# A third pair of k-tiles by seven products in ten of the eleven FFN blocks of a hybrid decoder kernel

## The chip, the cores and the metric

One core of one Trainium2 chip. The metric is device microseconds of one execution. The kernel before takes 1394.79 us, the median of three runs (1393.06 to 1396.41).

## What is computed

One layer: a pre-norm, a combined input projection, differential attention beside a state-space branch, a gated merge, an output projection, and then the feed-forward part (FFN) that the change touches. All is float32; x is 256 tokens by 2048, the FFN is 5632 wide.

```
z = _rms_norm(h, norm_ffn_pre[l])
f = (jax.nn.silu(z @ w_ffn_gate[l]) * (z @ w_ffn_up[l])) @ w_ffn_down[l]
h = h + _rms_norm(f, norm_ffn_post[l])
```

## The kernel before

**Split matmuls.** TensorE works on float32r. Each operand is held as a high part and a low part, and each product is three matmuls of 128x128 by 512 columns: high by high, high by low, low by high. The split of a weight tile is a CAST on ScalarE (`hi`) and a subtraction on VectorE (`lo`).

**FFN blocks.** The 5632 columns are eleven blocks of 512, `ffn0` to `ffn10`. A block multiplies z (two token tiles, 16 k-tiles of 128) by a 128x1024 weight tile per k-tile: 512 columns of gate, 512 of up. A plain k-tile (kind `D`) takes four products, 12 matmuls.

**Pairs by seven products.** In `ffn1` to `ffn10` two neighbouring k-tiles, with the two token tiles and the two column halves, can be seen as a 2x2 by 2x2 block product, and that can be done with seven products in place of eight (21 matmuls in place of 24), if sums of the blocks are made first. The sums of z are made once, by `combos`, near the end of `ffn0`. The sums of the weights are made in each block by `do_sums` on VectorE: one subtraction of 1024 columns (t1 and t3), then t2 and t4 of 512. A pair is four entries of the list `SETS`: `R2` (second tile), `B1` (first half of the first tile), `T13` and `T24` (the sums), in this order. P1 to P7 are the products' accumulators. Since plain k-tiles feed the same accumulators, a plain tile is a product each into P4, P5, P2 and P3, with the difference of the two token tiles of z (`hold["cd"]`) for P3.

**Buffers.** A pair's two weight tiles land in `ga[:, 1]`, and there is one such buffer; the sums go to `ga[:, 0]`, also one. A new pair isn't loaded before the last pair's `B1` has been split (`state["pair"]`), and what of the buffer is free is loaded at once, so the first quarter goes behind the first sum and the last behind `B1` or t4. Plain tiles land in four `raw` buffers. There are five pairs of `hi` and `lo` buffers, and the splits run up to four entries ahead of the products (`ensure`). All these copies are issued by SyncE (SP).

**Order.** The code is written in one order, but in the FFN blocks (`unpin`) a scheduler orders each engine's instructions at build time; each engine then runs its own list in order. Accumulators of odd and of even blocks lie in different PSUM banks (`s_alloc`), so the order differs between the two and repeats every two blocks. At a block's end `s_evac` adds the accumulators up on VectorE (seven adds of 512 columns) with two gate products behind a SiLU on ScalarE; `hid_t` transposes the result on TensorE.

Of the kernel before, what the change touches and what calls it, by code (L numbers as in the profile page):

```python
# [89 lines left out]
def hybrid_block_kernel(  # L90
# [52 lines left out]
    def big8(dtype=F32, shape=(P, 2048)):  # L143
        return b8.tile(list(shape), dtype, tag="b8", name=nm("b8"))
# [297 lines left out]
    hold = {}  # L442
# [540 lines left out]
    def add(*a, **kw):  # L983
        b = Block(*a, **kw)
        if b.order is None:
            b.order = bank_order(b.nk)
        blocks.append(b)
        return b
# [246 lines left out]
    def zf(t):  # L1235
        return ga[:, t].rearrange("p a (k n) -> p (a k) n", n=P)

    def combos(cb):

        if cb == 0:  # L1240
            cs = big8(F32R, (P, 2, 4, 2, P))
            hold["cs"], hold["cd"] = (cs[:, 0], cs[:, 1]), [big8(F32R, (P, 16, P)) for _ in range(2)]
        z0, z1 = zf(0), zf(1)
        n = 2 if cb % 2 else 4
        k0, k1, k2 = 4 * cb, 4 * cb + 2, 4 * cb + 3
        tt = V.tensor_tensor
        (ch, cl), (dh, dl) = hold["cs"], hold["cd"]
        tt(z1[:, k0:k0 + n], z0[:, k0:k0 + n], z1[:, k0:k0 + n], op=ALU.subtract)
        parts = [(z1[:, k0:k0 + n], dh[:, k0:k0 + n], dl[:, k0:k0 + n])]
        if n == 2:  # L1250
            tt(z1[:, k2], z1[:, k1], z1[:, k2], op=ALU.add)
            tt(z1[:, k1], z0[:, k1], z1[:, k1], op=ALU.subtract)
            tt(z0[:, k1], z1[:, k2], z0[:, k1], op=ALU.subtract)
            tt(z0[:, k2], z0[:, k2], z0[:, k1], op=ALU.subtract)
            parts += [(z1[:, k1:k1 + 2], ch[:, 0:2, cb // 2], cl[:, 0:2, cb // 2]),
                      (z0[:, k1:k1 + 2], ch[:, 2:4, cb // 2], cl[:, 2:4, cb // 2])]
        for src, h, l in parts:
            A.copy(h, src)
            tt(l, src, h.bitcast(F32), op=ALU.subtract)
# [53 lines left out]
    def load_ffn(b):  # L1313
        def f(k, r):
            for w, c0 in ((w_g, 0), (w_u, 512)):
                nc.sync.dma_start(r[:, :, c0:c0 + 512],
                                  w[k * P:(k + r.shape[1]) * P, b * 512:(b + 1) * 512].rearrange("(a p) c -> p a c", p=P))
        return f
# [33 lines left out]

    quad = lambda k: [(kind, k) for kind in ("R2", "B1", "T13", "T24")]
    plain = lambda *ks: [("D", k) for k in ks]
    SETS = plain(0, 1, 2, 3, 4) + quad(6) + plain(5, 8, 9, 10) + quad(14) + plain(11, 12, 13)
    USES = dict(D=(("P4", 0), ("P5", 1), ("P2", 0), ("P3", 1)), R2=(("P2", 0), ("P3", 1)), B1=(("P1", 0),),
                T13=(("P7", 1), ("P5", 0)), T24=(("P6", 0), ("P4", 1)))

    def s_mm(m, accs, h, l, first, last):
        n, key, c = m  # L1360
        kind, k = SETS[n]
        (ch, cl), (dh, dl) = hold["cs"], hold["cd"]
        z = lambda k_, t: tuple(zT[i][:, k_, t * P:(t + 1) * P] for i in "hl")
        q = k // 8
        if kind == "D":
            xh, xl = dict(P4=z(k, 1), P5=z(k, 1), P2=z(k, 0), P3=(dh[:, k], dl[:, k]))[key]
        elif key in ("P1", "P2", "P4"):
            xh, xl = dict(P1=z(k, 0), P2=z(k + 1, 0), P4=z(k + 1, 1))[key]
        else:
            i = dict(P7=0, P5=1, P6=2, P3=3)[key]  # L1370
            xh, xl = ch[:, i, q], cl[:, i, q]
        ps, sl = accs[key], slice(c * 512, c * 512 + 512)
        T.matmul(ps, xh, h[:, sl], start=first, stop=False)
        T.matmul(ps, xh, l[:, sl], start=False, stop=False)
        T.matmul(ps, xl, h[:, sl], start=False, stop=last)

    def s_alloc(b):
        def f():
            wide = side2()
            acc = lambda: acc_pool.tile([P, 512], F32, tag="acc", name=nm("acc"))  # L1380
            d = {}
            if b % 2:
                for key in ("P4", "P5", "P2", "P3"):
                    d[key] = acc()
                d["P1"], d["P6"], d["P7"] = side(), wide[:, 0, :], wide[:, 1, :]
            else:
                d["P4"], d["P5"], d["P2"] = wide[:, 0, :], wide[:, 1, :], side()
                for key in ("P1", "P6", "P7", "P3"):
                    d[key] = acc()
            return d  # L1390
        return f

    def s_evac(b):
        def f(key, accs):
            s0, s1, X, Y = (hold["sc"][:, 512 * n:512 * n + 512] for n in range(4))
            plus = lambda o, a, k_: V.tensor_tensor(o, a, accs[k_], op=ALU.add)

            def gated(t, g, u):
                A.activation(g, g, AF.Silu, scale=hold["rstd2"][:, t:t + 1])
                V.scalar_tensor_tensor(g, u, hold["rstd2"][:, t:t + 1], g, op0=ALU.mult, op1=ALU.mult)  # L1400
                hid[(b, t)] = g
            if key == "P1":
                A.copy(s0, accs["P1"])
            elif key == "P6":
                plus(X, s0, "P6")
                plus(Y, X, "P7")
            elif key == "P4":
                plus(s1, Y, "P4")
            elif key == "P5":
                plus(X, X, "P5")  # L1410
                plus(Y, Y, "P5")
                gated(1, s1, Y)
            elif key == "P2":
                plus(s0, s0, "P2")
            elif key == "P3":
                plus(X, X, "P3")
                gated(0, s0, X)
                tasks.append((f"hid{b}", hid_t(b)))
        return f

    every = [[(n, key, c) for key, c in USES[kind]] for n, (kind, _) in enumerate(SETS)]
    s_order = [st[:3] for st in every[:3]] + [[st[3] for st in every[:3]]] + every[3:-2]
    s_order.append([st[i] for i in range(4) for st in every[-2:]])
    for b in range(1, NB):
        add(f"ffn{b}", len(SETS), load_ffn(b), None, s_evac(b), budget=0.6, mm=s_mm, alloc=s_alloc(b), order=s_order)
        blocks[-1].sets = SETS
        blocks[-1].akey = lambda m: m[1]

    def steps(*fs):
# [13 lines left out]
        9: steps((unpin,), (h_add, 1, 3), (h_piece, 0, 2), (h_square, 0, 0)),  # L1443
        10: steps((h_piece, 1, 2), (h_square, 1, 0)),
        11: steps((h_square, 0, 1), (combos, 0)),
        12: steps((h_piece, 0, 3), (h_square, 1, 1)),
        13: steps((h_piece, 1, 3), (h_square, 0, 2), (combos, 1)),
        14: steps((h_square, 1, 2), (h_square, 0, 3), (combos, 2)),
        15: steps((h_square, 1, 3), (norm2,), (combos, 3))}

# [131 lines left out]
```

## Time and profile before

| what | value |
|---|---|
| median of three runs | 1394.79 us |
| the profiled execution, its span | 1398.8 us, 1397.0 us |
| TensorE busy | 1356.9 us, 97% |
| VectorE busy | 1009.5 us, 72% |
| ScalarE busy | 722.6 us, 52% |
| granted TensorE clock, mean | 0.983 |

The span is what the profiler sees from the first to the last instruction. Engines are PE (TensorE), PEld (its weight loads), DVE (VectorE), ACT (ScalarE), POOL and SP. In the trace all instructions of the helper `InOrder` have line 41, so they are told apart by tiles. `lo<-raw,hi` is the split of a plain tile, `lo<-ga,hi` that of a pair's entry, `ga<-ga` of 1024 columns the first sum of a pair, `ga<-ga` of 512 one of the short sums, `b<-b,acc` and `b<-b,side` the adds at a block's end. Blocks `ffn1` to `ffn10` run from about 710 to 1137 us.

### The profile page before, as it was taken

The page shows a single profiled execution, that of the slowest core. Times are in us where ns is not written, and L with a number is a line of the kernel's source. Part 1 is how long each engine was busy: PE and PEld are TensorE (multiplying, and loading weights), DVE is VectorE, ACT ScalarE, POOL GpSimd, SP SyncE. Part 2 cuts the span into 40 slices and gives each one's busy share as a digit, 9 for nine tenths or more (in the row PEclk, how much of TensorE's full clock was granted, in tenths as well). Part 3 has the DMA queues.
Part 4 walks back from the last instruction along what each step waited for, and adds up shares of the span by engine and source line. Part 5 has one row for each costly group of instructions (what it writes and reads, how often), then busy time and mean ns, then how long its engine had stood idle before and what let it go on. Part 6 is the DMA issues. An engine that isn't in the chain of part 4 may idle for free.

```text
span 1397.0 us, 17778 instructions
## 1 busy us (share of the span) xinstructions
PE 1356.9 (97%) x6307; PEld 1104.5 (79%) x6307; DVE 1009.5 (72%) x1316; ACT 722.6 (52%) x1079; POOL 168.3 (12%) x187
## 2 busy tenths in 40 slices
PE   7999999999999989999999999999999999999997
PEld 6887777777777778888788888888888878888885
DVE  4954999868999956645976777767868676555555
ACT  3646545687545454544574555545555455444443
POOL 3090344302244100000000000000000000000001
PEclk8999999999999989999999999999999999999999
DMA  8678666544566556656566656566565566555551
GB/s 244 200 225 253 212 190 186 153 136 143 176 177 187 167 175 227 223 187 197 166 193 207 211 154 229 172 200 211 175 210 189 180 248 228 189 201 180 197 181 60
DMA packets 103577, 266.72 MB, mean 191 GB/s; under 512 B 11488, under 2 KB 18480, under 8 KB 100352
## 3 DMA queue, kind: packets, MB, share of 16 engines
q1 hardware_dynamic: 102272, 260.09, 58.5%
q10 hardware_dynamic: 608, 4.20, 0.8%
q0 software_dynamic: 608, 1.30, 0.4%
q8 instruction: 49, 0.80, 0.2%
q14 instruction: 40, 0.33, 0.1%
HBM read 257.16 MB, written 8.39 MB: 190 GB/s over the span
## 4 chain that ended last, share of the span: by engine, by line
issue 53%; PE 25%; DVE 13%; POOL 3%; ACT 3%; DMA 2%; SPq 1%; POOLq 0%; DVEq 0%; ACTq 0%
PE acc L41 23%; DVE lo L41 4%; PE side L41 2%; DVE ssB L41 2%; DVE ssD L41 2%; DVE ssA L41 2%; DVE ssC L41 1%; ACT hi L41 1%; DMA b<-in_x_dram 1%; SPq L668 1%; DVE ga L41 1%; DVE sim L41 1%; DVE b L41 1%; POOL tabS L685 1%; DVE sre L41 0%
## 5 line engine op out<-in xcount | busy, mean ns | idle before, releaser
L41 DVE TENSOR_TENSOR lo<-raw,hi 128x1024 fp32r<-128x1024 f32 (+1 forms) x385 | 473.6, 1240 | 163.7 <-ACT hi L41 163.0
L41 ACT CAST hi<-raw 128x1024 fp32r<-128x1024 f32 (+1 forms) x384 | 398.0, 1050 | 318.3 <-PE acc L41 220.1
L41 PE MATMUL acc<-hi,b 128*128 128x512 f32 x596 | 209.2, 394 | 0.4 <-DVE b L41 0.3
L41 PE MATMUL acc<-lo,xT_h 128*128 128x512 f32 x512 | 205.0, 404 | 2.6 <-DVE lo L41 2.5
L41 PE MATMUL acc<-hi,xT_l 128*128 128x512 f32 x512 | 202.4, 399 | 0.0
L41 PE MATMUL acc<-hi,xT_h 128*128 128x512 f32 x512 | 164.1, 406 | 5.3 <-ACT hi L41 3.5
L41 PEld LDWEIGHTS acc<-hi,b 128*128 128x128 f32 x596 | 112.4, 189 | 24.9 <-issue 0.8
L41 PEld LDWEIGHTS acc<-lo,xT_h 128*128 128x128 f32 x512 | 98.5, 193 | 28.1 <-DVE lo L41 5.1
L41 PEld LDWEIGHTS acc<-hi,xT_h 128*128 128x128 f32 x512 | 97.2, 193 | 28.4 <-ACT hi L41 6.2
L41 PE MATMUL acc<-lo,b 128*128 128x512 f32 x298 | 117.4, 394 | 2.1 <-DVE lo L41 2.1
L41 DVE TENSOR_TENSOR lo<-ga,hi 128x1024 fp32r<-128x1024 f32 x80 | 84.6, 1087 | 47.0 <-ACT hi L41 47.0
L41 ACT CAST hi<-ga 128x1024 fp32r<-128x1024 f32 x80 | 72.7, 943 | 82.1 <-PE acc L41 71.5
L41 PEld LDWEIGHTS acc<-hi,xT_l 128*128 128x128 f32 x512 | 98.3, 192 | 19.6
L41 PE MATMUL acc<-lo,zT_h 128*128 128x512 f32 x274 | 105.8, 392 | 0.4 <-DVE lo L41 0.4
L41 PE MATMUL acc<-hi,zT_l 128*128 128x512 f32 x274 | 105.1, 390 | 0.0
L41 PE MATMUL acc<-hi,zT_h 128*128 128x512 f32 x274 | 95.4, 393 | 0.2 <-ACT zT_h L41 0.2
L41 DVE TENSOR_TENSOR ga<-ga 128x512 f32<-128x512 f32 (+4 forms) x85 | 60.5, 716 | 35.4 <-DMA ga<-in_w_ffn_gate_dram 32.2
L439 POOL TENSOR_TENSOR rstdf<-rstdfm,half 128x1 f32<-128x1 f32 x2 | 1.1, 547 | 675.3 <-DVE rstdfm L41 675.3
L41 PE MATMUL side<-lo,zT_h 128*128 128x512 f32 x210 | 82.1, 391 | 0.0
L41 PE MATMUL side<-hi,zT_l 128*128 128x512 f32 x210 | 81.8, 389 | 0.0
L41 PE MATMUL side<-hi,zT_h 128*128 128x512 f32 x210 | 77.7, 389 | 0.0
L41 DVE TENSOR_TENSOR lo<-b,hi 128x1024 fp32r<-128x1024 f32 x40 | 49.0, 1225 | 39.0 <-ACT hi L41 39.0
(230 smaller groups left out, 2326.7 us busy)
## 6 DMA issues: line engine op xcount, KB each, us to landing
raw<-in_w_in_dram SPq DMA_DIRECT2D x127, 512.0 KB, 4.2
raw<-in_w_ffn_gate_dram SPq DMA_DIRECT2D x136, 256.0 KB, 3.7
raw<-in_w_ffn_up_dram SPq DMA_DIRECT2D x136, 256.0 KB, 4.0
raw<-in_w_ffn_down_dram SPq DMA_DIRECT2D x48, 512.0 KB, 4.3
b<-in_w_ffn_down_dram SPq DMA_DIRECT2D x20, 1024.0 KB, 4.9
raw<-in_w_out_dram SPq DMA_DIRECT2D x32, 512.0 KB, 4.1
ga<-in_w_ffn_gate_dram SPq DMA_DIRECT2D x40, 256.0 KB, 3.7
ga<-in_w_ffn_up_dram SPq DMA_DIRECT2D x40, 256.0 KB, 3.0
```

The costliest lines, as they stand in the source:

```text
L41: ins = f(*a, **kw)
L439: G.tensor_tensor(r, ms, half[:, :n], op=ALU.pow)
L668: nc.sync.dma_start(stack_b[:, j // 2, n, :, j % 2].rearrange("g q o n -> q g o n"), t_[32 * j:32 * j + 32])
L685: G.tensor_tensor(up(tss), hi(sa), lo(cb), op=ALU.mult)
```

## The change

`SETS` makes k-tiles 10 and 11 a third pair in `ffn1` to `ffn10` and moves the plain tiles around the pairs. Its sums of z need a place: they go into slots 6, 7, 14 and 15 of the differences `hold["cd"]`, which no plain tile uses. `combos` makes them, and its second call of four columns of tiles becomes two differences and four sums.

```diff
+    def sums_of(k, i, n, part):
+
+        if k == 10:
+            return hold["cd"][part][:, (6, 7, 14, 15)[i]:(6, 7, 14, 15)[i] + n]
+        return hold["cs"][part][:, i:i + n, k // 8]
+
     def combos(cb):
...
-        n = 2 if cb % 2 else 4
+        n = 2 if cb else 4
...
-            parts += [(z1[:, k1:k1 + 2], ch[:, 0:2, cb // 2], cl[:, 0:2, cb // 2]),
-                      (z0[:, k1:k1 + 2], ch[:, 2:4, cb // 2], cl[:, 2:4, cb // 2])]
+            for i, src in ((0, z1), (2, z0)):
+                parts.append((src[:, k1:k1 + 2], sums_of(k1, i, 2, 0), sums_of(k1, i, 2, 1)))
...
-    SETS = plain(0, 1, 2, 3, 4) + quad(6) + plain(5, 8, 9, 10) + quad(14) + plain(11, 12, 13)
+    SETS = (plain(0, 1, 2, 3) + quad(6) + plain(4, 5) + quad(10) + plain(8, 9) + quad(14)
+            + plain(12, 13))
...
-        q = k // 8
...
-            xh, xl = ch[:, i, q], cl[:, i, q]
+            xh, xl = (sums_of(k, i, 1, part)[:, 0] for part in (0, 1))
```

Each engine's order moves with it. In the rows, every name carries a number of its own; `lo` of 1024 columns out of `raw` is the split of a plain tile, out of `ga` that of a pair's entry. VectorE in `ffn2`, the first even block, before the change:

```order
L41 TENSOR_TENSOR ga<-ga 128x1024
L41 TENSOR_TENSOR lo_6898<-raw_6719,hi_6897 128x1024
L41 TENSOR_TENSOR lo_6911<-raw_6781,hi_6910 128x1024
L41 TENSOR_TENSOR lo_6924<-ga,hi_6923 128x1024
L41 TENSOR_TENSOR ga<-ga 128x512
L41 TENSOR_TENSOR lo_6943<-ga,hi_6942 128x512
L41 TENSOR_TENSOR ga<-ga 128x512
L41 TENSOR_TENSOR lo_6965<-ga,hi_6964 128x1024
L41 TENSOR_TENSOR ga<-ga 128x1024
L41 TENSOR_TENSOR lo_6984<-ga,hi_6983 128x1024
```

These are the first sum of pair 14, tiles 9 and 10, `R2`, t2, `B1`, t4, `T13`, then the first sum of the next block's pair 6, and `T24` of pair 14. VectorE in the same block of the changed kernel:

```order
L41 TENSOR_TENSOR ga<-ga 128x1024
L41 TENSOR_TENSOR lo_6867<-raw_6702,hi_6866 128x1024
L41 TENSOR_TENSOR lo_6877<-raw_6715,hi_6876 128x1024
L41 TENSOR_TENSOR ga<-ga 128x512
L41 TENSOR_TENSOR lo_6884<-ga,hi_6883 128x1024
L41 TENSOR_TENSOR lo_6894<-ga,hi_6893 128x512
L41 TENSOR_TENSOR lo_6914<-ga,hi_6913 128x1024
L41 TENSOR_TENSOR ga<-ga 128x512
L41 TENSOR_TENSOR ga<-ga 128x1024
L41 TENSOR_TENSOR lo_6933<-ga,hi_6932 128x1024
L41 TENSOR_TENSOR lo_6952<-raw_6822,hi_6951 128x1024
```

These are the first sum of pair 10, tiles 4 and 5, t2, `R2`, `B1`, `T13`, t4, then the first sum of pair 14 of the same block, `T24` of pair 10, and tile 8. What moved: the next pair's first sum, which stood ahead of a `T24` once in the block, at its last pair, now stands there at pair 10.

TensorE at the end of `ffn2`, before: the end of the last product into P5 (`side`), then a plain tile of `ffn3` (`hi_7068`) and the first row of tile 3 (`hi_7072`), whose low part is first read three rows below the last one shown:

```order
L41 MATMUL side_1282_6775<-lo_7022,zT_h 128x512
L41 MATMUL side_1282_6775<-hi_7021,zT_l 128x512
L41 MATMUL acc_7122<-hi_7068,zT_h 128x512
L41 MATMUL acc_7122<-lo_7069,zT_h 128x512
L41 MATMUL acc_7122<-hi_7068,zT_l 128x512
L41 MATMUL acc_7123<-hi_7068,zT_h 128x512
L41 MATMUL acc_7123<-lo_7069,zT_h 128x512
L41 MATMUL acc_7123<-hi_7068,zT_l 128x512
L41 MATMUL acc_7124<-hi_7068,zT_h 128x512
L41 MATMUL acc_7124<-lo_7069,zT_h 128x512
L41 MATMUL acc_7124<-hi_7068,zT_l 128x512
L41 MATMUL acc_7122<-hi_7072,zT_h 128x512
```

And at the same place of the changed kernel (`hi_7086` is tile 3 of `ffn3`, `lo_7087` its low part):

```order
L41 MATMUL side_1282_6783<-lo_7047,zT_h 128x512
L41 MATMUL side_1282_6783<-hi_7046,zT_l 128x512
L41 MATMUL acc_7136<-hi_7086,zT_h 128x512
L41 MATMUL acc_7137<-hi_7086,zT_h 128x512
L41 MATMUL acc_7138<-hi_7086,zT_h 128x512
L41 MATMUL acc_7136<-lo_7087,zT_h 128x512
L41 MATMUL acc_7136<-hi_7086,zT_l 128x512
```

What moved: between the last product into P5 and the first read of tile 3's low part there were twelve matmuls, and there are three.

## Rows read from the trace of the kernel before

**Rows 1.** The page's first part: busy us, share of the span, instructions.

```profile
PE 1356.9 (97%) x6307; PEld 1104.5 (79%) x6307; DVE 1009.5 (72%) x1316; ACT 722.6 (52%) x1079; POOL 168.3 (12%) x187
```

**Rows 2.** Windows of two FFN blocks each.

```profile
core 0: us, PE busy (x) PEld busy (x) DVE busy (x) ACT busy (x) POOL busy (x), PEclk, DMA share, GB/s
...
863.51:949.74 86.23, 86.23 (x390) 71.40 (x389) 64.95 (x72) 44.34 (x50) 0.00 (x0) 1.00 0.60 195
949.74:1035.97 86.23, 86.23 (x390) 71.39 (x389) 64.88 (x71) 44.34 (x50) 0.00 (x0) 1.00 0.61 195
```

**Rows 3.** Waits from 863.51 to 949.74: who waited for whom.

```profile
engine line waited for: us in total, times, longest us
...
DVE ga L41 <- DMA ga<-in_w_ffn_gate_dram: 7.6, 3, 3.3
...
DVE b L41 <- PE side L41: 3.8, 1, 3.8
...
PEld acc L41 <- DVE lo L41: 0.2, 1, 0.2
```

**Rows 4.** TensorE's timeline at the end of an even block: start, us, instruction.

```profile
889.22 0.39 PE L41 MATMUL acc<-hi,zT_h 128*128 128x512 f32 x1
...
891.03 0.39 PE L41 MATMUL side<-hi,zT_l 128*128 128x512 f32 x1
891.26 0.39 PE L41 MATMUL acc<-hi,zT_h 128*128 128x512 f32 x1
...
893.07 0.39 PE L41 MATMUL acc<-hi,zT_l 128*128 128x512 f32 x1
893.30 0.84 PE L41 MATMUL acc<-hi,zT_h 128*128 128x512 f32 x3
893.98 0.46 PE L41 MATMUL acc<-lo,zT_h 128*128 128x512 f32 x1
```

**Rows 5.** VectorE's timeline, instructions that follow without a wait.

```profile
878.68 2.35 DVE L41 TENSOR_TENSOR lo<-raw,hi 128x1024 fp32r<-128x1024 f32 x2
880.95 0.68 DVE L41 TENSOR_TENSOR b<-b,acc 128x512 f32<-128x512 f32 x1
881.55 1.22 DVE L41 TENSOR_TENSOR lo<-raw,hi 128x1024 fp32r<-128x1024 f32 x1
...
894.39 0.74 DVE L41 SCALAR_TENSOR_TENSOR b<-b,rstdh 128x512 f32<-128x512 f32 x1
895.06 1.22 DVE L41 TENSOR_TENSOR lo<-raw,hi 128x1024 fp32r<-128x1024 f32 x1
```

**Rows 6.** Windows: the end of ffn0, and one with TensorE partly idle.

```profile
680.00:720.00 40.00, 40.00 (x188) 32.77 (x188) 35.37 (x54) 27.01 (x47) 1.64 (x1) 1.00 0.70 219
...
1120.00:1160.00 40.00, 38.85 (x176) 31.91 (x174) 29.09 (x32) 19.60 (x23) 0.00 (x0) 1.00 0.69 248
```

**Rows 7.** VectorE's timeline: B1's split, and the sum that waited behind it.

```profile
781.71 0.69 DVE L41 TENSOR_TENSOR lo<-ga,hi 128x512 fp32r<-128x512 f32 x1
...
786.85 1.23 DVE L41 TENSOR_TENSOR ga<-ga 128x1024 f32<-128x1024 f32 x1 [2.43 <-DMA ga<-in_w_ffn_gate_dram]
...
825.35 0.69 DVE L41 TENSOR_TENSOR lo<-ga,hi 128x512 fp32r<-128x512 f32 x1
...
831.70 1.23 DVE L41 TENSOR_TENSOR ga<-ga 128x1024 f32<-128x1024 f32 x1 [4.20 <-DMA ga<-in_w_ffn_gate_dram]
...
868.65 0.68 DVE L41 TENSOR_TENSOR lo<-ga,hi 128x512 fp32r<-128x512 f32 x1
...
873.94 1.23 DVE L41 TENSOR_TENSOR ga<-ga 128x1024 f32<-128x1024 f32 x1 [2.56 <-DMA ga<-in_w_ffn_gate_dram]
...
912.01 0.68 DVE L41 TENSOR_TENSOR lo<-ga,hi 128x512 fp32r<-128x512 f32 x1
...
917.79 1.23 DVE L41 TENSOR_TENSOR ga<-ga 128x1024 f32<-128x1024 f32 x1 [3.32 <-DMA ga<-in_w_ffn_gate_dram]
```

**Rows 8.** VectorE's timeline at the end of an even block: the adds of P5.

```profile
891.46 1.29 DVE L41 TENSOR_TENSOR b<-b,side 128x512 f32<-128x512 f32 x2 [3.80 <-PE side L41]
892.66 1.22 DVE L41 TENSOR_TENSOR lo<-raw,hi 128x1024 fp32r<-128x1024 f32 x1
```

**Rows 9.** SP's timeline: copies of a pair issued.

```profile
868.79 0.33 SPq L1316 DMA_DIRECT2D ga<-in_w_ffn_up_dram  x1
869.36 0.93 SPq L1316 DMA_DIRECT2D ga<-in_w_ffn_gate_dram  x2
```

## The prediction

> **What bounds the kernel now.** I read the page, then windows laid from one pair sum to the fourth after it, then each engine's timeline there. The page has TensorE busy 97% and VectorE 72% [rows 1], but that is a mean over stages; the change touches the FFN stage only. Two FFN blocks take 86.23 us there, TensorE is busy in all of it at a granted clock of 1.00 (2.4 GHz), and VectorE has 64.95 us of work [rows 2]. The reader should see in the waits of that stretch that TensorE waited 0.2 us in all, while VectorE waited three times, 7.6 us together, for the copies of a pair [rows 3]. So TensorE sets the pace, but one loop runs close beside it: the sums of a pair read the only pair buffer, the next pair's copies start when the split of B1 has let it go, and the next sums wait for the landing.
>
> **What goes.** A pair kept plain is two k-tiles of 12 matmuls, a pair by seven products is 21. Every block goes from 186 to 183. From the start at 889.22 to that at 893.07 there are 17 matmuls [rows 4], 0.2265 us each, so 0.68 us a block and 6.8 us in ten. If nothing else changed, two blocks would take 84.9 us.
>
> **What comes, on the engines.** VectorE: instructions that follow each other without a wait start 1.135 us apart for 1024 columns (two from 878.68 to 880.95), 0.60 for 512 and 0.67 for a gate product [rows 5]. Two plain splits go (2.27) and four splits (3 x 1.135 + 0.60) and three sums (1.135 + 2 x 0.60) come: 4.07 us more a block. Before it is 12 plain splits (13.62), two pairs (12.68), seven adds (4.20) and two gate products (1.34), 31.8 us; after, 35.9 of TensorE's 42.4. By its sum alone VectorE still fits. ScalarE has 22.2 us of work a block, half of 44.34 [rows 2], gets some 1.6 us more, my estimate for four casts (one of half size) in place of two, and doesn't decide. The additional combinations of z in ffn0 are some 1.0 us of VectorE work (eight short operations for two of 512); ffn0 has it under a TensorE that is busy all of 40.00 us with VectorE at 35.37 [rows 6]. Nothing is charged; without that cover it is 1.0 us, once.
>
> **What comes, in the loop.** This is the term that decides. There is one buffer for a pair and one for its sums, and three pairs a block must now go through them. From the start of B1's split to the start of the next pair's first sum, where that sum waited, the rows give 5.14, 6.35, 5.29 and 5.78 us [rows 7]: 0.60 for the split itself, and the rest issue, flight and landing. I take the mean, 5.6, as these are the waits that the loop will have; 5.1 and 6.4 are the bounds.
>
> The order of VectorE in the changed kernel then gives six legs from first sum to first sum over two blocks; in each I add what stands ahead of B1's split.
> Even block, pair 6 to 10: the sum, two plain splits, a short sum and R2 are 5.14, and with 5.6 it is 10.74. Pair 10 to 14: here the next sum stands ahead of T24's split of pair 10, so T24, two plain splits, R2, the sum and two short sums are 6.88, leg 12.48.
> Odd block, pair 6 to 10: the same 10.74. Pair 10 to 14: the sum, two plain splits, two short sums and R2 are 5.74 ahead of B1, leg 11.34.
> The two long legs run from pair 6's sum of the next block, taken early, to that block's pair 10, over the block's end. VectorE's own work in one is 15.8 (eight operations of 1024, nine of 512, two gate products), so 21.4 with the copies. Two waits for TensorE make it longer:
> - Even to odd: VectorE must add P5 out of PSUM before it splits the new block's tile 3. D12's split ends 2.36 us into the leg (if TensorE is waiting for it, as I take it), TensorE's P5 ends 48 matmuls of its order (10.87) later, the first add starts 0.2 behind it (891.26 to 891.46) [rows 4, 8]; two adds, that split, an add, two gate products and R2 are 5.41. B1 starts at 18.84, leg 24.44. TensorE meets tile 3 earlier than before: from the end of P5 to the use of that split took 2.72 us (891.26 to 893.98) [rows 4], which 12 matmuls filled; three are left, so TensorE stalls some 2.0 us.
> - Odd to even: B1 is the sixth split of a block on five buffers. It waits until TensorE is through with tile 0, whose P2 product comes 65 matmul times (14.8) behind D12, whose split ends at 3.0. With a 0.6 cast B1 starts at 18.4, leg 24.0.
> The six are 10.74 + 12.48 + 24.44 + 10.74 + 11.34 + 24.0 = 93.7 us for two blocks, where now it is 86.2: 7.5 more, with the 0.68 a block already lost in it. The first block's first sums hang on ffn0 and the last has no pair behind it, so I count nine blocks of ten, 4.5 times 7.5, 34 us. The profiled execution took 1398.8 us (span 1397.0), which gives 1433; the median of the runs is 4.0 lower, and I forecast **1429 us**. With 5.1 for the copies six legs are 90.7 and the time 1415; with 6.4 they are 98.5 and it is 1450.
>
> One more price has been looked up. A quarter megabyte was issued at 869.36 and the sum that waited for it began 4.6 us later, at 873.94 [rows 7, 9]. The Trainium skill, DMA: Bandwidth & Descriptors, section "Anatomy of one DMA", gives 2.0 us and the bytes over 436 GB/s, an estimate of 2.6 us for this copy, fitted on another issuing path; the trace does not agree where several copies were issued close together. By it the loop would be hidden, which is the first rival below.
>
> **The rivals.**
> - *The copies stop mattering, and the matmuls saved come back* (faster). With holds as above the six legs fall to TensorE's 84.9 once B1-to-sum is 4.1 us or less, and to today's 86.2 at 4.35. For it: the three waits of VectorE for copies are 2.5 us each today on the mean of [rows 3], and a copy alone could be quicker. Against: no wait in these rows is under 5.1. Time 1394.8 - 6.8 = 1388. The rule of the Trainium skill in "Anatomy of one DMA" would give this too. Chance 0.10.
> - *The loop without the two holds.* If VectorE is never kept by P5 and tile 0, the long legs are 21.4 each, the six 88.0, 1.8 more for two blocks: 8 us, 1403. For it: a TensorE that waits more at other places is not where I put it. Against: today VectorE already waits 3.8 us for P5 [rows 3]. Chance 0.17.
> - *No change*: about 4.5 us a copy with the holds, or 5.3 without. Chance 0.06.
> - *The clock falls* because TensorE now pauses 1 to 3 us at a time. In a stretch with 1.15 us of 40 idle the granted clock stayed 1.00 [rows 6], and pauses of 9 in 94 us lie far from an idle engine. At half clock even a tenth of the FFN stage would cost over 40 us. Chance 0.02.
>
> **How the numbers follow.** The forecast, loop and holds, has 0.65. Slower by over 0.2% (2.8 us, about what a measurement of this kernel can tell) is it, the loop alone and the clock: 0.84. Same 0.06, faster 0.10. The range takes in the loop alone at its low side and the dear copies at the high: 1402 to 1452; below it lie the faster and the same, above it copies dearer than 6.4 or further waits.
>
> **What would show it.** Right: TensorE has 183 matmuls a block, and yet fourth sum to first sum (now six legs) takes about 94 us. VectorE's wait for the pair copies goes from 7.6 to some 15 us in two blocks, at six places in place of three, and TensorE, which waits 0.2 us there, waits about 9 for splits: at T24 of pair 10, tile 12 and tile 3. Wrong: a TensorE that is still busy throughout with two blocks at 84.9, or B1-to-sum under 4.4 us. If the block period is longer but the waits for copies stay at 7 to 8, my mechanism is wrong even with the sign right. What I trust least is the holds, worked out as if each began where the row order puts it.

## The result and the profile after

The changed kernel takes 1412.88 us (median of four runs, 1412.35 to 1413.93), the kernel before 1395.6 us beside it. The ratio is 1.0129, with a 95% interval of 1.0115 to 1.0142: 17.3 us slower. That lies in the range given (1402 to 1452) and on the side that was forecast, 16 us under the forecast of 1429.

The page's first part, which answers to [rows 1]:

```profile
PE 1357.3 (96%) x6277; PEld 1095.9 (78%) x6277; DVE 1051.9 (75%) x1372; ACT 737.3 (52%) x1101; POOL 165.7 (12%) x187
```

TensorE has 30 matmuls fewer, as foreseen, VectorE 56 instructions and 42 us more. Windows of two blocks each, from a first sum of a pair to the sixth behind it, in the columns of [rows 2]:

```profile
770.48:861.34 90.86, 87.06 (x383) 69.63 (x383) 73.01 (x81) 47.37 (x55) 0.00 (x0) 1.00 0.60 186
861.34:952.61 91.27, 88.45 (x384) 71.06 (x383) 72.91 (x80) 47.07 (x55) 0.00 (x0) 0.98 0.58 185
952.61:1041.72 89.11, 86.23 (x384) 69.97 (x383) 73.18 (x80) 47.20 (x55) 0.00 (x0) 1.00 0.60 189
1041.72:1130.99 89.27, 86.72 (x384) 69.88 (x383) 72.91 (x81) 47.04 (x55) 0.00 (x0) 1.00 0.60 189
```

Two blocks take 90.1 us on the mean, where they took 86.23: 3.9 more, and 4.5 times that is 17.6 us, the whole loss. At the pace of before (86.23 us for 390 matmuls) the 384 would take 84.9, so TensorE stands idle or slowed for 5.2 us in two blocks. The prediction had about 9 for it. The waits of the first window, against [rows 3]:

```profile
DVE ga L41 <- DMA ga<-in_w_ffn_gate_dram: 8.8, 5, 2.6
...
PEld acc L41 <- DVE lo L41: 3.5, 4, 1.5
DVE b L41 <- PE side L41: 3.4, 1, 3.4
```

VectorE's waits for pair copies have hardly grown: 8.8 us here, 7.6 before, and in the other three windows 5.3 to 5.6. The prediction had named 15, and had said that its mechanism is wrong if they stay at 7 to 8. By its own sign, then, the mechanism doesn't stand as it was stated, and which part of the loss the copies are had to be measured. VectorE's timeline of that window has the six legs (a group's start is that of its first instruction; the second of a `lo<-ga,hi` group that begins with R2 is B1):

```profile
770.48 1.23 DVE L41 TENSOR_TENSOR ga<-ga 128x1024 f32<-128x1024 f32 x1
...
774.50 2.96 DVE L41 TENSOR_TENSOR lo<-ga,hi 128x1024 fp32r<-128x1024 f32 x3
...
780.06 1.23 DVE L41 TENSOR_TENSOR ga<-ga 128x1024 f32<-128x1024 f32 x1 [2.00 <-DMA ga<-in_w_ffn_gate_dram]
...
786.95 2.96 DVE L41 TENSOR_TENSOR lo<-ga,hi 128x512 fp32r<-128x512 f32 x3
792.46 1.22 DVE L41 TENSOR_TENSOR ga<-ga 128x1024 f32<-128x1024 f32 x1 [2.55 <-DMA ga<-in_w_ffn_gate_dram]
...
801.68 1.28 DVE L41 TENSOR_TENSOR b<-b,side 128x512 f32<-128x512 f32 x2
806.35 1.29 DVE L41 TENSOR_TENSOR b<-b,side 128x512 f32<-128x512 f32 x2 [3.39 <-PE side L41]
807.55 1.22 DVE L41 TENSOR_TENSOR lo<-raw,hi 128x1024 fp32r<-128x1024 f32 x1
...
812.13 0.69 DVE L41 TENSOR_TENSOR lo<-ga,hi 128x512 fp32r<-128x512 f32 x1 [0.30 <-ACT hi L41]
...
816.16 1.23 DVE L41 TENSOR_TENSOR ga<-ga 128x1024 f32<-128x1024 f32 x1 [0.56 <-DMA ga<-in_w_ffn_gate_dram]
...
820.18 1.82 DVE L41 TENSOR_TENSOR lo<-ga,hi 128x1024 fp32r<-128x1024 f32 x2
...
826.13 1.23 DVE L41 TENSOR_TENSOR ga<-ga 128x1024 f32<-128x1024 f32 x1 [1.10 <-DMA ga<-in_w_ffn_gate_dram]
...
830.75 4.09 DVE L41 TENSOR_TENSOR lo<-ga,hi 128x1024 fp32r<-128x1024 f32 x4
837.44 1.95 DVE L41 TENSOR_TENSOR ga<-ga 128x1024 f32<-128x1024 f32 x2 [2.60 <-DMA ga<-in_w_ffn_gate_dram]
...
857.82 0.69 DVE L41 TENSOR_TENSOR lo<-ga,hi 128x512 fp32r<-128x512 f32 x1 [4.36 <-ACT hi L41]
```

The sums start at 770.48, 780.06, 792.46, 816.16, 826.13, 837.44 and 861.34. So the legs are 9.58, 12.40, 23.70, 9.97, 11.31 and 23.90; forecast were 10.74, 12.48, 24.44, 10.74, 11.34 and 24.0. (The prediction names the short legs one pair too early. The first and fourth run from pair 10 to pair 14, the second and fifth from pair 14 to the next block's pair 6.) Where TensorE waited in the even block of that window, and what it did ahead of the last two waits:

```profile
782.48 0.50 PE L41 MATMUL acc<-lo,b 128*128 128x512 f32 x1 [0.42 <-DVE lo L41]
...
794.87 0.50 PE L41 MATMUL side<-lo,zT_h 128*128 128x512 f32 x1 [0.73 <-DVE lo L41]
...
804.79 0.39 PE L41 MATMUL side<-hi,zT_h 128*128 128x512 f32 x1
...
805.24 0.39 PE L41 MATMUL side<-hi,zT_l 128*128 128x512 f32 x1
...
805.92 0.39 PE L41 MATMUL side<-hi,zT_l 128*128 128x512 f32 x1
806.81 0.96 PE L41 MATMUL acc<-hi,zT_h 128*128 128x512 f32 x3 [0.50 <-ACT hi L41]
808.82 0.50 PE L41 MATMUL acc<-lo,zT_h 128*128 128x512 f32 x1 [1.05 <-DVE lo L41]
```

These are the three places named ahead: T24 of pair 10, tile 12, and tile 3 behind P5. Tile 3 is the largest. From 805.92 to 806.81 and on to 808.82 TensorE makes four steps of 0.2265 in 2.90 us, so 2.0 us are lost, the very figure of the prediction. But its cause has two parts. At 805.24 the last matmul that reads tile 12's weights starts (its third into P5; tile 13's three follow), and only then ScalarE casts tile 3, into the buffers that tile 12 leaves:

```profile
805.71 1.05 ACT L41 CAST hi<-raw 128x1024 fp32r<-128x1024 f32 x1 [1.98 <-PE side L41]
```

VectorE's adds of P5 run from 806.35, and the split follows at 807.55 without a pause. The cast was done by 806.76, so what ended last is the adds, as predicted; but a split whose cast starts so late can only stand behind them. The way from tile 12's last matmul to the first read of tile 3's low part, 805.24 to 808.82, is 3.58 us. Before, 16 matmuls of the list lay in it (3.62 us), and now 7.

The odd block has three more places, none of them in the prediction:

```profile
840.58 0.50 PE L41 MATMUL acc<-lo,zT_h 128*128 128x512 f32 x1 [0.39 <-DVE lo L41]
...
845.88 0.47 PE L41 MATMUL side<-hi,zT_h 128*128 128x512 f32 x1 [0.47 <-DVE b L41]
...
854.85 1.03 PE L41 MATMUL side<-ident,b 128*128 128x128 f32 x8
856.12 0.50 PE L41 MATMUL side<-hi,zT_h 128*128 128x512 f32 x1 [0.24 <-ACT hT L41]
```

Counted from start to start, the late starts of the window are 0.6 us at T24, 0.9 at tile 12, 2.0 at tile 3, then 0.5, 0.6 and 0.5: 5.1 in all.

### The profile page after: what moved, and what is told of

The parts are those of the page before. It is cut to its first block, busy times and chain, and to the rows that moved or that the text cites. A ratio compares the mean times of both kernels' runs of the same rounds, so it can differ in the third digit from the quotient of the medians.

```text
span 1410.9 us, 17839 instructions
## 1 busy us (share of the span) xinstructions
PE 1357.3 (96%) x6277; PEld 1095.9 (78%) x6277; DVE 1051.9 (75%) x1372; ACT 737.3 (52%) x1101; POOL 165.7 (12%) x187
## 4 chain that ended last, share of the span: by engine, by line
issue 54%; PE 25%; DVE 13%; POOL 3%; ACT 3%; DMA 2%; SPq 1%; POOLq 0%; DVEq 0%; ACTq 0%
PE acc L41 23%; DVE lo L41 3%; PE side L41 2%; DVE ssB L41 2%; DVE ssD L41 2%; DVE ssA L41 2%; DVE ssC L41 1%; ACT hi L41 1%; SPq L668 1%; DVE sim L41 1%; DVE ga L41 1%; DMA b<-in_x_dram 1%; DVE b L41 1%; DVE sre L41 1%; DMA raw<-in_w_ffn_up_dram 0%
## 5 line engine op out<-in xcount | busy, mean ns | idle before, releaser
L41 DVE TENSOR_TENSOR lo<-raw,hi 128x1024 fp32r<-128x1024 f32 (+1 forms) x365 | 451.6, 1244 | 155.7 <-ACT hi L41 154.9
L41 ACT CAST hi<-raw 128x1024 fp32r<-128x1024 f32 (+1 forms) x364 | 377.7, 1050 | 325.6 <-PE acc L41 234.6
L41 DVE TENSOR_TENSOR lo<-ga,hi 128x1024 fp32r<-128x1024 f32 (+1 forms) x120 | 126.8, 1087 | 32.5 <-ACT hi L41 32.3
L41 ACT CAST hi<-ga 128x1024 fp32r<-128x1024 f32 (+1 forms) x120 | 110.4, 943 | 77.5 <-DVE ga L41 29.5
L41 DVE TENSOR_TENSOR ga<-ga 128x512 f32<-128x512 f32 (+4 forms) x119 | 87.3, 737 | 34.3 <-DMA ga<-in_w_ffn_gate_dram 29.6
L41 PE MATMUL acc<-hi,zT_l 128*128 128x512 f32 x259 | 100.7, 392 | 0.0
L41 PE MATMUL acc<-hi,zT_h 128*128 128x512 f32 x259 | 88.8, 396 | 2.2 <-ACT hi L41 2.0
L41 PE MATMUL side<-lo,zT_h 128*128 128x512 f32 x195 | 76.6, 393 | 2.8 <-DVE lo L41 2.8
L41 PE MATMUL side<-hi,zT_h 128*128 128x512 f32 x195 | 73.7, 395 | 2.6 <-DVE b L41 1.5
L41 PE MATMUL side<-hi,zT_l 128*128 128x512 f32 x195 | 76.1, 390 | 0.0
```

The source lines that it names most:

```text
L41: ins = f(*a, **kw)
```

## The experiments

Three theories stood against each other. The *loop theory* is mine: the copies into the one pair buffer and three sums a block. By the *order theory* the new order of entries costs by itself. By the *list theory* it is VectorE's longer list, whatever the copies do. Each window named below is of two blocks, in the order of the columns above.

**e1: the order alone.** Tiles 10 and 11 plain, in the third pair's place.

```diff
-    SETS = plain(0, 1, 2, 3, 4) + quad(6) + plain(5, 8, 9, 10) + quad(14) + plain(11, 12, 13)
+    SETS = (plain(0, 1, 2, 3) + quad(6) + plain(4, 5, 10, 11, 8, 9) + quad(14)
+            + plain(12, 13))
```

> Two pairs as before the change, but the entries in the changed kernel's order: 10 and 11 stay plain tiles, in the place where the third pair stands. The loop theory (the one pair buffer, its copies and three sums a block set the block's length): four sums in two blocks as before, so about 86.2 us for two blocks and 1395 us, within 4. The order theory (the new order costs by itself, since tile 3 is read three matmuls behind the last product into P5): the stall at tile 3 stays, some 2.1 us at the end of each even block, five times, so 1405 us. The list theory (what costs is VectorE's longer list, 73 us in two blocks where it was 65, with its waits for P5 and for casts, whatever the copies do): about 1395 us too, as VectorE's work is that of before.

Measured: 1403.72 us, ratio 1.0060 (1.0048 to 1.0072). The window:

```profile
857.48:945.62 88.14, 86.97 (x389) 71.30 (x388) 65.61 (x70) 44.28 (x51) 0.00 (x0) 1.00 0.60 191
```

Two pairs, VectorE's 65.6 us, and 1.9 us more than before. TensorE meets tile 3's low part too early here as well:

```profile
893.80 0.50 PE L41 MATMUL acc<-lo,zT_h 128*128 128x512 f32 x1 [0.93 <-DVE lo L41]
```

So 8.5 us of the loss come with the order of entries, without a third pair. The order theory is right as far as that goes, and the loop theory can't be all.

**e2 and e3: no wait for copies.** In e2 pairs behind `ffn1` aren't copied, so its output is another. In e3 they are, into two buffers in turn; the second lies in a part of `hT` that is still unused.

```diff
-                for a, r in enumerate(pair):
+                for a, r in enumerate(pair if blk.name == "ffn1" else []):
                     blk.load(kk + a, r)
```

The main part of e3's edit (`...` marks lines left out, where places that named the one buffer take the pair's own):

```diff
+    def take(blk):
+        j = next(j for j in free if j == 0 or blk.name != "ffn10")
+        free.remove(j)
+        used.append(j)
+        return ga[:, 1] if j == 0 else hold["hT"][:, 36:44].rearrange("p (a k) n -> p a (k n)", a=2)
...
-            do_sums()
-            state["pair"] = False
+            do_sums(blk.pairs[kk])
+            free.append(used.pop(0))
```

> The changed kernel without the copies of pairs behind ffn1: all later pairs use again what lies in the pair buffer, so the output is another. All sums, splits and matmuls stay. The loop theory: VectorE waits for no copy (5 to 9 us in two blocks now), most of TensorE's 5 us of stalls in two blocks go, two blocks take 84.9 to 86.5 us and the kernel 1388 to 1396 us. The list theory: the waits turn up again as waits for P5 and casts, two blocks stay at 89 to 91 us and the kernel at 1408 to 1414 us. The order theory: only the stalls at tile 3 are left, some 2 us in two blocks, so 1398 to 1402 us.

> The changed kernel with a second buffer for a pair, in ffn1 to ffn9, in the upper eighth of hT that those blocks don't write (hT slots 36 to 43); ffn10 has one buffer. Everything is computed and copied. The loop theory: a pair is copied while the last one is still read, so VectorE doesn't wait for copies, two blocks take 84.9 to 86.5 us and the kernel 1388 to 1397 us. The list theory: 1408 to 1414 us. The order theory: 1398 to 1402 us, with the stall at tile 3 left.

Measured: 1403.26 us without copies (ratio 1.0061, 1.0048 to 1.0075), 1402.43 with two buffers (1.0054, 1.0041 to 1.0068). The window and a wait of e3:

```profile
855.45:942.90 87.45, 85.66 (x383) 70.22 (x382) 72.96 (x82) 47.51 (x55) 0.00 (x0) 1.00 0.62 193
```

```profile
DVE b L41 <- PE side L41: 5.5, 1, 5.5
```

No wait for a pair copy is left in either, and some 10 us come back. That is what the loop costs: 90.1 to 87.45 in two blocks, 2.7 us. VectorE has 72.96 us of work there as well, so by the list theory nothing should have come back. But 7 us of the loss stay, with VectorE's wait for P5 at 5.5 us, longer than the 3.8 of [rows 3]. The stall at tile 3 stays too, at 889.92 (0.50) and 891.93 (1.05). The order theory had named 1398 to 1402 us for both runs, and is nearest.

**e4 to e7: tile 12 done with earlier.** The last two plain tiles of a block one after the other, not their products in turn. Between tile 12's last read and tile 3's low part TensorE's list then has some 40 matmuls.

```diff
-    s_order = [st[:3] for st in every[:3]] + [[st[3] for st in every[:3]]] + every[3:-2]
-    s_order.append([st[i] for i in range(4) for st in every[-2:]])
+    s_order = [st[:3] for st in every[:3]] + [[st[3] for st in every[:3]]] + every[3:]
```

> Two pairs in the changed kernel's order (as in the run before), but a block's last two plain tiles one after the other, not their products in turn: tile 12 is done with nine matmuls earlier, and P5's last product comes up to six matmuls later. The slot theory: tile 3's cast waits for the hi and lo buffers that tile 12 leaves (the fifth entry before it), the way from there to TensorE's first read of tile 3's low part is some 3.6 us, and the 11 matmuls of the order between the two hide 2.5 of them; now 41 stand there, so the stall of 1.2 us at each even block's end goes: 1395 us, within 4. The adds theory (VectorE adds P5 out of PSUM ahead of tile 3's split, which is what I predicted): P5 ends later, so the stall stays or grows, 1403 to 1410 us.

> The changed kernel with the same edit: tile 3's low part is first read 40 matmuls behind the last read of tile 12, where it was 7. The slot theory: the stall of 2.1 us at each even block's end goes; if the loop through the one pair buffer then isn't next, 1403 us (9 to 10 back); if it is, the time goes to VectorE's waits for copies and it stays between 1403 and 1413 us. The adds theory: 1412 us or more.

> The changed kernel with two pair buffers and the same edit: both suspected waits gone. If these two are all that costs, TensorE is left with its 384 matmuls in two blocks, 84.9 us and half a us at the transposes: 85.4 us, and the kernel 1388 to 1393 us, faster than before the change. The adds theory: 1402 us. If VectorE's longer list is what costs: over 1397 us.

> The kernel before the change with the same edit, as a control: TensorE waits 0.2 us in two blocks there, so by every theory no change, 1395 us within 3; if the edit itself makes a block end better or worse (the gate products come later), it shows here.

Measured, as ratios to before:

| kernel | us | ratio, interval |
|---|---|---|
| e4, order alone | 1399.48 | 1.0031, 1.0019 to 1.0043 |
| e5, the change | 1414.52 | 1.0140, 1.0127 to 1.0154 |
| e6, two buffers | 1399.32 | 1.0031, 1.0019 to 1.0043 |
| e7, before | 1396.17 | 1.0010, 1.0001 to 1.0018 |

The slot theory missed. Half of e1's loss comes back, 3 of e3's 7 us, and nothing at all with one pair buffer. Its rival, the adds theory, named e5's time (1412 us or more) but missed e4 and e6 as well. The cast in e6 shows why with three pairs (e5 has the same wait, 1.18 us at 901.15), and TensorE's next matmul:

```profile
891.52 1.04 ACT L41 CAST hi<-ga 128x1024 fp32r<-128x1024 f32 x1 [5.53 <-PE side L41]
```

```profile
892.62 0.50 PE L41 MATMUL acc<-hi,zT_h 128*128 128x512 f32 x1 [1.01 <-ACT hi L41]
```

The hold has moved one entry on. Now it is R2 of pair 6 that wants the buffers which tile 13 leaves, and tile 13 ends as late as before. So the question was why the last products of a block stand so late in TensorE's list. The list of the changed kernel answers it, with the waits of each entry (`side_1282_6783` is the PSUM tile of two banks that holds P4 and P5 of the even block; `hi_7036` is tile 12, `hi_7046` tile 13, `hi_7086` tile 3 of the next block):

```
L41 MATMUL side_1282_6783<-hi_7036,zT_h 128x512 [waits DVE_49]
L41 MATMUL side_1282_6783<-lo_7037,zT_h 128x512
L41 MATMUL side_1282_6783<-hi_7036,zT_l 128x512
L41 MATMUL side_1282_6783<-hi_7046,zT_h 128x512
L41 MATMUL side_1282_6783<-lo_7047,zT_h 128x512
L41 MATMUL side_1282_6783<-hi_7046,zT_l 128x512
L41 MATMUL acc_7136<-hi_7086,zT_h 128x512 [waits Activation_49]
```

P5's last products wait for VectorE although tile 12 has been read by TensorE before: they wait for the add of P4, which reads the other bank of the same tile. In the built list 27 matmuls of the next block stand ahead of them, where before the change there were 18; that the scheduler reckoned the add late is the likely reason, but nothing here shows it. The engine runs its list in order. The add is the second of the two from 801.68, so it was done by 803, yet the products run only from 804.79.

**e8 to e11: the add of P4 out of the way.** It is written behind P5's last product, so that P5 doesn't wait for it.

```diff
-            elif key == "P4":
-                plus(s1, Y, "P4")
             elif key == "P5":
+                plus(s1, Y, "P4")
                 plus(X, X, "P5")
```

> Two pairs in the changed kernel's order, and one line moved: the add of P4 is written behind P5's last product, with the adds of P5, not ahead of it. P4 and P5 of an even block lie in one PSUM tile of two banks, and P5's last two products (tiles 12 and 13) have a wait for VectorE's add of P4 in their list entry, so in the list of TensorE the next block's tiles 0 to 2 stand ahead of them. With the line moved 38 matmuls stand between tile 12's last read and tile 3's low part in place of 11. The bank theory (this wait is the root of the stall at tile 3, and with it of what the order costs): 1395 us within 3. If the order costs otherwise: 1400 to 1404 us.

> The changed kernel with the add of P4 moved in the same way; one pair buffer. The bank theory and the loop theory together: the stall at tile 3 goes (some 2 us in two blocks), the loop through the one pair buffer stays or becomes the next bound: 1400 to 1410 us. If the loop alone sets the block's length, no change: 1412 to 1415 us.

> The changed kernel with two pair buffers in ffn1 to ffn9 and the add of P4 moved: both causes taken away. TensorE is left with 384 matmuls in two blocks, 84.9 us, and half a us at the transposes: 1388 to 1392 us, faster than before the change. If VectorE's longer list costs by itself: 1396 us or more.

> The kernel before the change with the add of P4 moved, as a control: TensorE waits 0.2 us in two blocks there, so there is nothing to win: 1395 us within 3 by every theory.

Measured:

| kernel | us | ratio, interval |
|---|---|---|
| e8, order alone | 1397.02 | 1.0014, 1.0005 to 1.0024 |
| e9, the change | 1405.80 | 1.0072, 1.0059 to 1.0085 |
| e10, two buffers | 1391.96 | 0.9980, 0.9971 to 0.9990 |
| e11, before | 1393.00 | 0.9985, 0.9977 to 0.9994 |

The windows of e8, e9, e10 and e11, in this order:

```profile
941.47:1028.39 86.92, 86.68 (x389) 71.41 (x388) 65.65 (x71) 44.29 (x51) 0.00 (x0) 1.00 0.61 194
```

```profile
860.63:948.82 88.19, 85.94 (x384) 70.02 (x383) 72.99 (x80) 46.91 (x55) 0.00 (x0) 1.00 0.61 191
```

```profile
850.75:936.07 85.32, 85.08 (x383) 70.39 (x382) 72.72 (x81) 47.38 (x55) 0.00 (x0) 1.00 0.64 198
```

```profile
944.52:1030.66 86.14, 86.14 (x390) 71.48 (x389) 64.93 (x72) 44.44 (x50) 0.00 (x0) 1.00 0.61 196
```

Of the order's 8.5 us 6 to 7 come back, of the change's 17.3 as many, and with two buffers 10, more than the 7 that were left there. VectorE's wait for P5 is gone from the windows of e8, e9 and e10. In e9 TensorE no longer waits at tile 3, but still at T24 of pair 10, at tile 12, at a first product that waits for VectorE's adds (933.36), and behind the transposes (943.58):

```profile
872.83 0.50 PE L41 MATMUL acc<-lo,b 128*128 128x512 f32 x1 [0.60 <-DVE lo L41]
...
885.30 0.50 PE L41 MATMUL side<-lo,zT_h 128*128 128x512 f32 x1 [0.84 <-DVE lo L41]
...
933.36 0.47 PE L41 MATMUL side<-hi,zT_h 128*128 128x512 f32 x1 [0.58 <-DVE b L41]
...
943.58 0.50 PE L41 MATMUL side<-hi,zT_h 128*128 128x512 f32 x1 [0.24 <-ACT hT L41]
```

With a second pair buffer (e10) all but the last of these go. Two blocks take 85.32 us, as expected (85.4), with VectorE at 72.7 us of them. So VectorE's longer list costs nothing by itself, and the list theory is out. Splitting P4 and P5 over two PSUM tiles, which would also take the wait away, was not tried.

The wait behind the transposes came with the order too. In the new list tile 0's first product into P2, which waits for a copy of `hT` out of PSUM, stands right behind the last transpose; in the list of before, at least five matmuls stand between. It is in e1, e3, e8 and e10, and in neither the kernel before nor e11. The eight transposes and the next product, before the change:

```profile
939.39 1.04 PE L41 MATMUL side<-ident,b 128*128 128x128 f32 x8
940.18 0.47 PE L41 MATMUL side<-lo,zT_h 128*128 128x512 f32 x1
```

From the first transpose to that product it is 0.79 us. In the changed kernel it is 1.27 (854.85 to 856.12, shown above), so 0.5 us more in two blocks: most of the 0.7 by which e8's window (86.92) is still above the 86.23 of before.

e10 is 0.2% faster than the kernel before. The control e11 gained 0.15%, so the runs don't tell how much of e10's 2.5 us is the third pair. By the windows it is 0.8 us in two blocks (86.14 to 85.32), some 3.7 us in nine blocks, and the profiled executions are 4.3 us apart (1391.98 and 1387.72). But e10's is the fastest of its twelve runs, and by the medians the two are only 1.0 us apart.

## Why the prediction was right, and where not

**Matmuls and VectorE's work: right.** 384 matmuls in two blocks in place of 390, and VectorE's 64.9 us became 73.0: 4.05 a block, forecast 4.07.

**What stands ahead of B1 in the short legs: right.** Forecast were 5.14, 6.88, 5.14 and 5.74 us. From 780.06 to 786.95 it is 6.89. In the other three B1 starts 1.135 behind R2: 775.63, 821.32 and 831.88, so 5.15, 5.16 and 5.75.

**The copies: the mis-sized term.** I took 5.6 us from B1's split to the next sum in all six legs, the mean of four waits. In the window it is 4.43, 5.51, 4.03, 4.81, 5.56 and 3.52, mean 4.64: 5.7 us less over six legs. The two long ones (4.03, 3.52) have nearly no wait for copies, since T13 and T24 stand ahead of the sum and the copies land while these run, or 0.6 us after. So the forecast of waits at six places and 15 us fell as well: there are five, 8.8 us, and less in the other windows. The legs with holds gave 2.8 us of it back (B1 starts 19.67 and 20.38 into them, forecast 18.84 and 18.4). Together 93.7 - 5.7 + 2.8 = 90.8, and the window has 90.86. So there was luck in the time: four of the six legs lie under 5.1, the prediction's lower bound for this term, and by its sum the measured 4.64 with the holds as forecast gives 88.0 us for two blocks, some 1403 us, at the very end of the range. Holds that were sized too small put 10 us back.

How long a copy of a pair's quarter takes isn't one number. From issue to landing these three took 3.2, 2.7 and 4.4 us:

```profile
778.08 0.33 SPq L1322 DMA_DIRECT2D ga<-in_w_ffn_gate_dram  x1
...
811.19 0.33 SPq L1322 DMA_DIRECT2D ga<-in_w_ffn_gate_dram  x1
...
832.85 0.42 SPq L1322 DMA_DIRECT2D ga<-in_w_ffn_gate_dram  x1
```

In the 4.4 us ahead of each, SyncE had issued four, two and six other copies, in this order, so the time goes with how many are under way; no run takes that apart. The sum at 837.44 began 4.59 us behind the third of them. (The sum at 780.06 doesn't wait for the copy of 778.08, which lands at 781.3, but for the one issued at 776.35, 3.7 us ahead of it.)

From the Trainium skill, DMA: Bandwidth & Descriptors, section "Anatomy of one DMA", an estimate of 2.6 us follows for a quarter of a megabyte, on the GpSimd path. Only the copy of 811.19 comes near that and the one of 832.85 takes far longer, so a loop of several copies isn't to be sized by it.

**"The term that decides" was half of it.** Without copy waits (e3) 10 of 17 us come back, and the rest isn't in the loop. The hold at the end of an even block was put down to VectorE's adds of P5 ahead of tile 3's split. Its size was right (2.0 us) and its place too, and in the changed kernel the adds are what ended last. What lies behind them is TensorE's list, which the prediction read but did not explain: P5's last products stand 27 matmuls too late, for a wait on the add of P4 in the same PSUM tile, so that both the adds and, through the five buffers of split weights, tile 3's cast come late. It costs 2.1 us in two blocks with two buffers (e3 to e10, 87.45 to 85.32) and 2 with one (90.1 to about 88.1 over e9's three windows of 88.19, 88.91 and 87.15). The copies cost 2.7 with that wait (90.1 to 87.45) and 2.8 without (88.1 to 85.32). The two add up: 84.9 for the matmuls, 2.1 for the list, 2.7 for the copies and 0.4 at the transposes (e10's 85.32) make 90.1. The late starts of the first window say the same: 2.0 us at tile 3, 0.5 behind the transposes and 2.6 at the four other places, which are those that a second buffer takes away. Of the 5.2 us, then, about half is the copies and half is the list: the wait at tile 3 and the one behind the transposes.

**The hold at tile 0** (odd to even) is the leg of 23.9. B1's split waits 4.36 us there for its cast, at 857.82. In ScalarE's list the copies of `hT` stand ahead of that cast, and the cast itself waits for the third matmul of tile 0 into P2:

```profile
855.48 1.07 ACT L41 COPY hT<-side 128x512 f32<-128x512 f32 x2 [4.92 <-PE side L41]
857.17 2.71 ACT L41 CAST hi<-ga 128x512 fp32r<-128x512 f32 x3 [0.61 <-ACT hT L41]
```

```profile
856.69 0.40 PE L41 MATMUL side<-hi,zT_l 128*128 128x512 f32 x1
```

The copies end at 856.55, that matmul at 857.09, and the cast starts at 857.17. So tile 0 sets it, as predicted. It came 2.0 us later than forecast, of which some 1.6 are TensorE's own late starts on the way (840.58, 845.88 and 856.12). Two slips in the prediction's sums move nothing: 65 matmul times are 14.7 us, not 14.8, and six legs without holds are 88.1, not 88.0.

**The rivals.** Copies that stop mattering would give 1388. e10 is that case, bought with a second buffer and a moved line, at 1392. The loop without the two holds would give 1403, with long legs of 21.4; they are 23.7 and 23.9, so the holds are there. The clock that falls, at 0.02, did happen once in the profiled execution, for little (below).

## What to carry to other kernels

Before work is added to an engine that has a quarter of its time free, look for what it shares: a single buffer that is refilled between uses, and a PSUM tile in which one bank's reader holds up another bank's writer. Where lists are fixed at build time, the trace of before shows only what such a wait costs under today's cover; count the entries that lie between release and use (here 16 matmuls before, 7 after, for a way of 3.6 us), as those are what a longer list elsewhere takes away. And test by removing one wait at a time: here two causes of about equal size lay at different places, and either alone would have passed for the explanation.

## What the hardware showed that was not expected

TensorE's clock fell to its lower level for some 3 us behind a pause, seldom. Windows of e2 at the end of an even block (us, busy time of each engine, granted clock, DMA share, GB/s):

```profile
888.00:890.00 2.00, 0.95 (x4) 0.47 (x4) 2.00 (x4) 0.79 (x1) 0.00 (x0) 1.00 0.00 0
890.00:892.00 2.00, 2.00 (x7) 1.58 (x8) 2.00 (x3) 0.00 (x0) 0.00 (x0) 0.69 0.52 143
892.00:894.30 2.30, 2.30 (x7) 1.81 (x6) 0.91 (x2) 0.36 (x1) 0.00 (x0) 0.53 0.27 103
```

Matmuls start 0.43 us apart there in place of 0.2265, so 1.2 GHz and not 2.4, and some eight of them lose 1.7 us. It came three times in e2, once each in the changed kernel (900.7 to 903.6, in the second window of the result) and in e5, and in none of the other profiles between 700 and 1145 us, though e3 has the same pauses at tile 3 to the hundredth. What makes the difference stays open. In e2 it is the distance between its 89.07 us for two blocks (853.43 to 942.50) and the 87.45 of e3.
